# Fifty elementwise instructions move from GpSimd to VectorE, between the output projection and the first pair of the up projection

## The chip, the cores and the metric

The kernel runs on one core of one Trainium2 chip. The metric is device time of one execution in microseconds (us), the median of several runs. The profile shows one more execution, with a record of every instruction. "PE" is TensorE (matrix multiply), "PEld" its weight loads, "DVE" VectorE, "ACT" ScalarE, "POOL" GpSimd, "SP" the engine that issues the DMAs. Each engine takes its instructions strictly in the order of its own queue and stops at one whose operand isn't there yet.

## The reference, cut to what matters

One residual block over 1024 frames of width 1024, in float32:

```
h   = rmsnorm(x) * (1 + scale1(c)) + shift1(c)
x   = x + gate1(c) * (concat(ssd(h), shortconv(h)) @ w_out)     # output projection
h   = rmsnorm(x) * (1 + scale2(c)) + shift2(c)
u   = causal_dwconv(h @ w_up) + bias                            # up projection, 2 x 2816 wide
x   = x + gate2(c) * ((silu(g) * v) @ w_down)                   # g, v = halves of u
out = rmsnorm(x)
```

The change lies in the output projection, the norm behind it, and the start of the up projection.

## The kernel before, in words

**Precision and product.** A float32 product is made of three fast ones. Every operand is split into a high part and a low part (`split`, L112 to L117): ACT copies the source into the rounded high part (L116), then another engine subtracts it from the source, which is the low part (L117). `mm3` (L125 to L127) issues high x high, high x low and low x high. So each 128x512 piece of an operand costs one ACT copy and one subtraction, and PE waits for both.

**Strassen-like blocks.** The output projection and the up projection use seven products in place of eight (`sw_operands`, `product`, L1000 on; `prep`, L535 on). Their operands are sums and differences of blocks: `sub` (L387), `add` (L662), and in `prep` the lines L558 and L561.

**Output projection.** `product(m, 8, ring_o, ...)` walks over eight row blocks i; for each it splits two 128x512 operands (`operand`: one from the mixer's result, one from a weight page "raw"), and issues twelve matmuls. The order of the seven products is m1, m2, m6, m5, m3, m7, m4. In m1 and m2 the weight's subtraction is on GpSimd (`eng=nc.gpsimd`), in the others on VectorE; `m2` also puts one `sub` per block on GpSimd. `later`/`defer` spread other work over the products: loads, the gate (L1056), the squares for the norm, and in m7 the splits of `half0` (L1177), of which every second one is on GpSimd.

**Norm and transposes.** Behind the last product, tiles 4 to 7 of x get their gate (L1223), their sum of squares on ACT (L1142), a reciprocal root in about a dozen tiny VectorE instructions (`rsqrt`, L97 to L106), and a scaled copy (`x_norm`, L1156 to L1159). PE then transposes them (`f_tile`, L1165) and ACT moves them out of PSUM (L1167).

**Up projection.** 22 pairs p of a gate block and a value block. `prep_u(p)` returns a list of small steps on the pair's two weight pages: the sums S1 to S4 and seven splits. For pair 0 they run on GpSimd beside the norm, for pair 1 on VectorE, from pair 2 on the sums run on GpSimd and the splits on VectorE. The right operands T1, T2, T3, B22 and T4 are made once, by `put`, out of the transposed tiles; B22 and T4 are made on GpSimd. Then pair follows pair, each with its products, the causal convolution taps (L1309, L1330) and the product of gate and value (L1333). Beside the first pairs run the sums of the sixth modulation vector (L163), sixteen of them.

**What sets the order.** The code is recorded and a scheduler puts each engine's queue in order before the launch; `tc.high_priority` pulls a step forward. Weight pages come from rings of a few buffers: the DMA into a buffer is issued when its last reader is done.

Of the kernel before, what the change touches and what calls it, by code (L numbers as in the profile page):

```python
# [36 lines left out]
def block_kernel(ctx: ExitStack, tc: tile.TileContext, x, crow, w_adat, w_m, w_z, w_dt,  # L37
                 w_out, w_up, w_down, vecs, rows, fnw, consts, out):
    nc = tc.nc
# [14 lines left out]
    def nm(s):  # L54
        uid[0] += 1
        return f"{s}{uid[0]}"

    def big():
        return pg.tile([P, T], F32, tag="pg", name=nm("pg"))

    def bank():
        return ps.tile([P, 512], F32, tag="ps", name=nm("ps"))

    def hhalf(dt=F32R):
        return ph.tile([P, 512], dt, tag="H", name=nm("H"))

    def hpage():
        return hhalf(), hhalf()
# [7 lines left out]
    def halves(page):  # L76
        return page[:, 0:512], page[:, 512:]
# [35 lines left out]
    def split(hi, lo, src, scale=None, eng=None):  # L113

        if scale is None:
            nc.scalar.activation(hi, src, AF.Copy)  # L116
            (eng or nc.vector).tensor_tensor(lo, src, hi.bitcast(F32), op=ALU.subtract)  # L117
        else:
            nc.scalar.activation(hi, src, AF.Copy, scale=scale)
            nc.vector.scalar_tensor_tensor(lo, src, scale, hi.bitcast(F32), op0=ALU.mult,  # L120
                                           op1=ALU.subtract)
# [125 lines left out]
    for k in range(ND):  # L247
# [3 lines left out]
        for q in range(2):  # L251
            s = slice(q * 512, q * 512 + 512)
            o = bank()
# [42 lines left out]
    o = bank()  # L296
# [34 lines left out]
    o = bank()  # L331
# [7 lines left out]
    o = bank()  # L339
# [46 lines left out]
    def sub(o, i0, i1, eng=None):  # L386
        (eng or nc.vector).tensor_tensor(o, i0, i1, op=ALU.subtract)  # L387
# [130 lines left out]
    wts = {}  # L518

    def w_half():  # L520
        if cur[0] is None:
            n = npage[0]
            npage[0] += 1
            pool, nb = (pv[0], 1) if pv[0] and n % 5 == 4 else (pw, None)
            h, l = [pool.tile([P, 1024], F32R, tag=t, bufs=nb, name=nm(t)) for t in ("wh", "wl")]
            cur[0] = (h[:, 512:], l[:, 512:])
            return h[:, 0:512], l[:, 0:512]
        r, cur[0] = cur[0], None
        return r
# [242 lines left out]
    with tc.high_priority(offset=100):  # L772
        for f in w0:
            f()
        gs, vl = big(), bank()
# [68 lines left out]
    for p in range(1, NS):  # L844
# [3 lines left out]
        gs, vl = (big(), nxt_vl) if p > 1 else (gs1, vl1)  # L848
# [73 lines left out]
    def sc_pair(i, q):  # L922

        rt, s = halves(tpage()), slice(q * 512, q * 512 + 512)
        for h in range(2):
            j = 2 * i + h
            y = Y[8 + j][q]
            nc.sync.dma_start(y, yd[j][:, s])
            for g in range(2):
                nc.sync.dma_start(rt[h][g * 64:(g + 1) * 64, :],  # L930
                                  rd[2 * j + g, s].partition_broadcast(64))
            nc.vector.scalar_tensor_tensor(y, y, col(V_SN + j), rt[h], op0=ALU.mult, op1=ALU.mult)
# [3 lines left out]
    def sw_operands(Y, load, eng=None):  # L936

        def m1(i):
            return Y(i)[0], load(i, 0, 0), []

        def m2(i):
            gl, gr, vl, vr = Y(i)
            return vl, load(i, 0, 1), [lambda: sub(gl, gl, gr, eng), lambda: add(gr, gr, vr)]

        def m5(i):
            gl, gr, vl, vr = Y(i)
            return gr, load(i, 2, 0), [lambda: sub(gr, vr, gl)]

        def m6(i):
            gl, gr, vl, vr = Y(i)  # L950
            return gr, load(i, 3, 1), [lambda: sub(vl, vl, gr, eng)]

        def m3(i):
            return Y(i)[2], load(i, 1, 1), []

        def m7(i):
            return Y(i)[0], load(i, 3, 0), []

        def m4(i):
            return Y(i)[3], load(i, 2, 1), []  # L960
        return m1, m2, m5, m6, m3, m7, m4

    def acc_banks():
        return [bank() for c in range(4)]

    def big_banks():
        return [*halves(big()), *halves(big())]

    def operand(f, i, ring, eng=None):

        h, l = ring()
        a, w, after = f(i)
        split(h[:, 0:512], l[:, 0:512], a)
        split(h[:, 512:], l[:, 512:], w, eng=eng)
        for g in after:
            g()
        return h[:, 0:512], l[:, 0:512], h[:, 512:], l[:, 512:]

    def dmm(o, c, op, start, stop, more=False):
        ah, al, bh, bl = op  # L980
        cs = slice(c * P, (c + 1) * P)
        mm3(o, ah[:, cs], al[:, cs], bh, bl, start, stop, more)
# [3 lines left out]
    def defer(n):  # L986
        for _ in range(min(n, len(later))):
            later.pop(0)()

    def product(f, n, ring, o=None, i0=0, i1=None, pops=1, eng=None, more=False):  # L990

        o = o or acc_banks()
        for i in range(i0, n if i1 is None else i1):
            op = operand(f, i, ring, eng)
            for c in range(4):
                dmm(o[c], c, op, i == 0 and not more, i == n - 1, more)
            defer(pops)
        return o
# [13 lines left out]
    NM2 = 4  # L1012
# [6 lines left out]
    def fetch():  # L1019
        if not quarters:  # L1020
            return
        i, page, half = quarters.pop(0)
        if wq[0] is None:
            t, wq[0] = halves(rawpage())
        else:
            t, wq[0] = wq[0], None
        src = w_out[page, i] if page < 2 else tout[i][page - 2]
        nc.sync.dma_start(t, src[:, half * 512:half * 512 + 512])
        ahead.append(t)

    def load_o(i, page, half):
        fetch()
        return ahead.pop(0)

    def Yo(i):
        return Y[2 * i] + Y[2 * i + 1]

    m1, _, _, _, m3, m7, m4 = sw_operands(Yo, load_o)

    def m2(i):  # L1040
        gl, gr, vl, vr = Yo(i)
        return vl, load_o(i, 0, 1), [lambda: sub(gl, gl, gr, nc.gpsimd)]

    def m6(i):
        gl, gr, vl, vr = Yo(i)
# [13 lines left out]
    def hset():  # L1059
        return [hhalf(F32) for c in range(4)]  # L1060
# [39 lines left out]
    later += [lambda: ssd_load(1, (0, 1)), lambda: ssd_load(1, (2, 3)), last_pair]  # L1100
    later += [lambda: ssd_load(1, (4, 5)), lambda: ssd_load(1, (6, 7))]
    pgs = hhalf(F32)
    o = product(m1, 8, ring_o, i1=7, pops=2, eng=nc.gpsimd)
    later += [lambda i=i: sc_pair(i, 1) for i in range(3)]
    o2 = product(m2, 8, ring_o, big_banks(), i1=NM2, eng=nc.gpsimd)
    op = operand(m1, 7, ring_o)
    for c in range(4):
        dmm(o[c], c, op, False, True)
# [5 lines left out]
    for c in range(4):  # L1114
        nc.scalar.activation(acc[c], o[c], AF.Copy)
    oa = o
    o = product(m2, 8, ring_o, o2, NM2, eng=nc.gpsimd)
    c11 = hset()
    for c in range(4):
        add(c11[c], o[c], acc[c])  # L1120
# [40 lines left out]
    def f_tile(q, k):  # L1161

        o = bank() if q else big()[:, 0:512]
        for i in range(4):
            nc.tensor.transpose(o[:, i * P:(i + 1) * P], xn[4 * q + i][:, k * P:(k + 1) * P], ident)  # L1165
        f = yhalf()
        nc.scalar.activation(f, o, AF.Identity, scale=A2c[:, k:k + 1], bias=sh2[:, k:k + 1])  # L1167
        return f

    xn = [None] * NT  # L1170
    f0, f1 = [None] * ND, [None] * ND

    def half0(k):
        f0[k] = f_tile(0, k)
        o = OPS["B11" if k < 4 else "B21"]
        o[k % 4] = hpage()
        split(o[k % 4][0], o[k % 4][1], f0[k], eng=nc.gpsimd if k % 2 else nc.vector)  # L1177

    for c in range(4):
        later += [lambda c=c: gate(c12[c], c, 1), lambda c=c: x_norm(c)]  # L1180
# [17 lines left out]
    def prep_u(p):  # L1198
        def s3_tile():
            if p == 0:  # L1200
                return s3_first
            return pv[0].tile([P, 512], F32, tag="t3", bufs=1, name=nm("s3"))
        return prep(p, [w_up[2 * p], w_up[2 * p + 1]], s3_tile, p < 1,
                    nc.vector if p == 1 else nc.gpsimd, nc.gpsimd if p == 0 else None)

    w0 = prep_u(0)
    s3_first = yhalf()
# [4 lines left out]
    wts[1] = {}  # L1212
    for n, f in zip(("A11", "A12"), halves(t)):
        wts[1][n] = w_half()
        split(*wts[1][n], f, eng=nc.gpsimd)
    for f in w0[2:5]:
        f()
    w0 = w0[5:]
# [14 lines left out]
    def put(name, k, src, eng=None):  # L1233
        n = nput[0]
        nput[0] += 1
        if n < 8:
            d = hpage()
        elif n < 12:
            d = halves(tpage(F32R))
        elif n == 15:  # L1240
            d = small(F32R), small(F32R)
        else:
            d = yhalf(F32R), yhalf(F32R)
        OPS[name][k] = d
        split(d[0], d[1], src, eng=eng)
# [23 lines left out]
    w1 = prep_u(1)  # L1269
# [20 lines left out]
            put("T3", k, f1[k])  # L1290
        prod(V[0][0], "S3", "T3", 0, True, ks=[k])
    for k in range(4):
        put("B22", k, f1[k + 4], nc.gpsimd)
    for k in range(4):
        sub(f0[k + 4], f0[k + 4], f0[k], nc.gpsimd)
        put("T4", k, f0[k + 4], nc.gpsimd)
    hd = [pd.tile([P, T], F32, name=f"hd{p}") for p in range(NF - 1)]


# [66 lines left out]
    for p in range(NF):  # L1366
        nxt = w1 if p == 0 else prep_u(p + 1) if p + 1 < NF else sum(map(early_operand, range(3)), [])
        vl = V[p][0]
        if p > 1:
            G[p] = big()  # L1370
        gl, gr = halves(G[p])
# [34 lines left out]
    o = acc_banks()  # L1406
# [46 lines left out]
    m1, m2, m5, m6, m3, m7, m4 = sw_operands(Yd, load_d)  # L1453
# [17 lines left out]
    o = product(m1, NQ, ring, o, NE)  # L1471
# [4 lines left out]
    o = product(m2, NQ, ring)  # L1476
# [62 lines left out]
    o = product(m5, NQ, ring)  # L1539
# [3 lines left out]
    o = product(m6, NQ, ring)  # L1543
# [4 lines left out]
    o = product(m3, NQ, ring)  # L1548
# [4 lines left out]
    o = product(m7, NQ, ring)  # L1553
# [6 lines left out]
    o = product(m4, NQ, ring, [big()[:, 0:512], bank(), bank(), big()[:, 0:512]], i1=NQ - NL)  # L1560
# [87 lines left out]
```

## Time and profile before

| what | value |
|---|---|
| median of 3 runs | 1467.11 us (1466.14 to 1467.79) |
| profiled execution, device time | 1469.52 us |
| its span, first to last instruction | 1467.7 us |
| mean granted TensorE clock, share of full | 0.979 |
| busy: PE / DVE / ACT / POOL | 1388.9 / 1176.8 / 731.3 / 309.3 us |

A busy time is the sum of an engine's instructions. PE at 95% means that about 79 us of the span pass without a matmul. The chain of waits names what ended last at each moment; its share by engine is no busy share. An idle time in brackets, as `[6.16 <-ACT wh L116]`, stands in front of the row that it delayed, with the instruction that ended it.

### The profile page before, as it was taken

The numbers are of one execution on the slowest core, as the hardware profiler recorded it, in microseconds if no ns is written. First come the engines' busy times: TensorE is split into PE (matmuls) and PEld (weight loads), VectorE is DVE, ScalarE is ACT, GpSimd is POOL, SyncE is SP. The second block draws the span as 40 slices with busy tenths as digits, with TensorE's granted clock in tenths as the row PEclk, the third lists the DMA queues.
The fourth block names the chain that finished last, engine by engine and source line by source line (L and its number), as shares of the span: only waits on it lengthen the run. The fifth ranks groups of instructions, "written<-read, shape, count | busy, mean of one in ns | idle before, by whom it ended". The sixth has DMA issues, their size and how long they took to land.

```text
span 1467.7 us, 17850 instructions
## 1 busy us (share of the span) xinstructions
PE 1388.9 (95%) x6159; PEld 1113.9 (76%) x6159; DVE 1176.8 (80%) x1882; ACT 731.3 (50%) x1272; POOL 309.3 (21%) x213
## 2 busy tenths in 40 slices
PE   4999999999999999998998699999999999999997
PEld 2788876777777777876886477888888888888885
DVE  7988868978898785599489799777777776889688
ACT  6633365666544434344486453444444444545463
POOL 0000032322012322261014733332333330000000
PEclk9999999999999999999999799999999999999999
DMA  8878964336454431785335132222222222856322
GB/s 319 299 267 316 310 199 164 136 103 222 152 173 154 140 122 61 253 253 184 114 116 172 58 129 101 86 86 82 77 87 86 87 86 101 316 207 209 100 101 101
DMA packets 89723, 232.18 MB, mean 158 GB/s; under 512 B 10296, under 2 KB 11016, under 8 KB 89632
## 3 DMA queue, kind: packets, MB, share of 16 engines
q1 hardware_dynamic: 89584, 231.00, 45.9%
q8 instruction: 48, 0.79, 0.2%
q14 instruction: 43, 0.35, 0.1%
q10 hardware_dynamic: 48, 0.05, 0.0%
HBM read 178.93 MB, written 52.08 MB: 157 GB/s over the span
## 4 chain that ended last, share of the span: by engine, by line
PE 63%; DVE 19%; DMA 6%; issue 5%; ACT 4%; POOL 1%; SPq 0%; DVEq 0%; POOLq 0%; ACTq 0%
PE ps L125 11%; PE ps L126 11%; PE ps L127 11%; PE pg L125 8%; PE pg L126 8%; PE pg L127 8%; DVE wl L117 3%; PE ps L485 2%; DVE sm L835 1%; DMA sm<-in_w_adat 1%; DMA cmb<-in_w_down 1%; ACT wh L116 1%; DVE cmb L387 1%; DVE T L373 1%; PE ps L493 1%
## 5 line engine op out<-in xcount | busy, mean ns | idle before, releaser
L116 ACT ACTIVATE wh<-raw 128x512 fp32r<-128x512 f32 (+1 forms) x272 | 173.0, 656 | 263.6 <-POOL raw L561 142.9
L117 DVE TENSOR_TENSOR wl<-raw,wh 128x512 fp32r<-128x512 f32 (+1 forms) x252 | 212.3, 855 | 78.7 <-ACT wh L116 72.6
L125 PE MATMUL pg<-H,wh 128*128 128x512 f32 x464 | 185.8, 402 | 10.5 <-ACT wh L116 6.2
L127 PE MATMUL pg<-H,wl 128*128 128x512 f32 x464 | 184.0, 397 | 1.7 <-DVE wl L117 1.7
L126 PE MATMUL pg<-H,wh 128*128 128x512 f32 x464 | 184.8, 398 | 0.4 <-DVE H L117 0.4
L125 PEld LDWEIGHTS pg<-H,wh 128*128 128x128 f32 x464 | 88.8, 192 | 32.1 <-ACT wh L116 7.3
L125 PE MATMUL ps<-H,wh 128*128 128x512 f32 x272 | 109.1, 402 | 3.8 <-ACT u L1265 3.8
L558 POOL TENSOR_TENSOR s<-raw,raw 128x512 f32<-128x512 f32 x28 | 53.5, 1912 | 278.4 <-DVE wl L117 166.6
L126 PE MATMUL ps<-H,wh 128*128 128x512 f32 x272 | 109.1, 401 | 3.2 <-DVE H L117 3.2
L127 PE MATMUL ps<-H,wl 128*128 128x512 f32 x272 | 108.0, 397 | 1.5 <-DVE wl L117 1.5
L126 PE MATMUL ps<-rg,rg 128*128 128x512 f32 x274 | 106.8, 390 | 0.0
L127 PE MATMUL ps<-rg,rg 128*128 128x512 f32 x274 | 106.6, 390 | 0.0
L127 PEld LDWEIGHTS pg<-H,wl 128*128 128x128 f32 x464 | 88.7, 191 | 21.5 <-DVE wl L117 3.2
L125 PE MATMUL ps<-rg 128*128 128x512 f32 x274 | 104.8, 390 | 0.0
L126 PEld LDWEIGHTS pg<-H,wh 128*128 128x128 f32 x464 | 88.7, 191 | 20.8 <-DVE H L117 2.5
L561 POOL TENSOR_TENSOR raw<-raw 128x512 f32<-128x512 f32 x58 | 85.9, 1492 | 78.6 <-DVE wl L117 69.1
L116 ACT ACTIVATE rg<-hp 128x512 fp32r<-128x512 f32 x85 | 51.6, 626 | 66.3 <-PE ps L127 46.1
L117 DVE TENSOR_TENSOR rg<-hp,rg 128x512 fp32r<-128x512 f32 x85 | 56.9, 684 | 18.2 <-ACT rg L116 18.0
L1330 DVE SCALAR_TENSOR_TENSOR cv<-ps,vec,cv 128x511 f32<-128x511 f32 (+2 forms) x132 | 67.8, 564 | 1.5 <-ACT cv L1326 1.4
L1309 DVE SCALAR_TENSOR_TENSOR cv<-pg,vec,cv 128x1023 f32<-128x1023 f32 (+1 forms) x44 | 56.2, 1277 | 15.4 <-ACT cv L1304 15.4
L662 DVE TENSOR_TENSOR pg<-pg,u 128x512 f32<-128x512 f32 x68 | 47.2, 694 | 25.3 <-PE pg L127 24.9
L487 POOL TENSOR_TENSOR xq<-xq,rw 128x512 f32<-128x512 f32 x16 | 19.0, 1186 | 221.3 <-issue 134.2
(379 smaller groups left out, 3513.5 us busy)
## 6 DMA issues: line engine op xcount, KB each, us to landing
raw<-in_w_up SPq DMA_DIRECT2D x45, 512.0 KB
raw<-in_w_m SPq DMA_DIRECT2D x36, 512.0 KB
sm<-in_w_adat SPq DMA_DIRECT2D x48, 256.0 KB
hd<-cv SPq DMA_DIRECT2D x21, 512.0 KB
hp<-hd SPq DMA_DIRECT2D x21, 512.0 KB
wr<-tdn SPq DMA_DIRECT2D x33, 256.0 KB
bc<-in_w_adat SPq DMA_DIRECT2D x16, 512.0 KB
seg<-ccd SPq DMA_DIRECT2D x16, 512.0 KB
```

The costliest lines, as they stand in the source:

```text
L116: nc.scalar.activation(hi, src, AF.Copy)
L117: (eng or nc.vector).tensor_tensor(lo, src, hi.bitcast(F32), op=ALU.subtract)
L125: nc.tensor.matmul(o, ah, bh, start=start, stop=False, skip_group_check=more)
L126: nc.tensor.matmul(o, ah, bl, start=False, stop=False, skip_group_check=more)
L127: nc.tensor.matmul(o, al, bh, start=False, stop=stop, skip_group_check=more)
L485: nc.tensor.matmul(y[:, h * HD:(h + 1) * HD], seg[:, h, :], xd[:, h * HD:(h + 1) * HD], start=True, stop=True)
L487: nc.gpsimd.tensor_tensor(hv(xg), hv(xg), rw[:, 2, g * 8:g * 8 + 8].unsqueeze(2).to_broadcast([P, 8, HD]), op=ALU.mult)
L558: sums.tensor_tensor(s3[0], a11, a21, op=ALU.subtract)
L561: return lambda: sums.tensor_tensor(o, i0, i1, op=op)
L662: nc.vector.tensor_tensor(o, i0, i1, op=ALU.add)
L1309: nc.vector.scalar_tensor_tensor(t[:, i:], g[:, :T - i], col(V_FW + (2 - i) * 44 + j), t[:, i:], op0=ALU.mult, op1=ALU.add)
L1330: nc.vector.scalar_tensor_tensor(o, v, col(V_FW + (2 - i) * 44 + j), o, op0=ALU.mult, op1=ALU.add)
```

## The change

Fifty instructions of shape 128x512 go from GpSimd's queue to VectorE's: in the output projection fifteen splits of weights and eight differences in `m2` (four of these eight belong to the product's second call); four splits of `half0`; four sums and seven splits of the weights of pairs 0 and 1; four splits of B22; four differences and four splits for T4. Nothing else is computed, and no amount of data changes. Besides, the first five steps of pair 1's list (its sums and its splits S2 and S1) are called ahead of the steps that make T4. (The list counts pairs from 0; the change's title calls pair 1 the second pair.)

```diff
     def m2(i):
         gl, gr, vl, vr = Yo(i)
-        return vl, load_o(i, 0, 1), [lambda: sub(gl, gl, gr, nc.gpsimd)]
+        return vl, load_o(i, 0, 1), [lambda: sub(gl, gl, gr)]
...
-    o = product(m1, 8, ring_o, i1=7, pops=2, eng=nc.gpsimd)
+    o = product(m1, 8, ring_o, i1=7, pops=2)
...
-    o2 = product(m2, 8, ring_o, big_banks(), i1=NM2, eng=nc.gpsimd)
+    o2 = product(m2, 8, ring_o, big_banks(), i1=NM2)
...
-    o = product(m2, 8, ring_o, o2, NM2, eng=nc.gpsimd)
+    o = product(m2, 8, ring_o, o2, NM2)
...
-        split(o[k % 4][0], o[k % 4][1], f0[k], eng=nc.gpsimd if k % 2 else nc.vector)
+        split(o[k % 4][0], o[k % 4][1], f0[k])
...
         return prep(p, [w_up[2 * p], w_up[2 * p + 1]], s3_tile, p < 1,
-                    nc.vector if p == 1 else nc.gpsimd, nc.gpsimd if p == 0 else None)
+                    nc.vector if p < 2 else nc.gpsimd)
...
-        split(*wts[1][n], f, eng=nc.gpsimd)
+        split(*wts[1][n], f)
...
     for k in range(4):
-        put("B22", k, f1[k + 4], nc.gpsimd)
+        put("B22", k, f1[k + 4])
+    for f in w1[:5]:
+        f()
+    w1 = w1[5:]
     for k in range(4):
-        sub(f0[k + 4], f0[k + 4], f0[k], nc.gpsimd)
-        put("T4", k, f0[k + 4], nc.gpsimd)
+        sub(f0[k + 4], f0[k + 4], f0[k])
+        put("T4", k, f0[k + 4])
```

The queues show where the moved instructions come to stand. VectorE in product m2 of the output projection (wl is a low part, H and ys hold the mixer's result, raw a weight page; - is before, + is now):

```order
 L117 TENSOR_TENSOR wl_5415<-raw_5264,wh_5414 128x512
-L662 TENSOR_TENSOR ys_5058<-ys_5058,ys_5060 128x512
 L117 TENSOR_TENSOR wl_5455<-ys_5047,wh_5454 128x512
+L117 TENSOR_TENSOR wl_5455<-raw_5307,wh_5454 128x512
 L932 SCALAR_TENSOR_TENSOR ys_5046<-ys_5046,vec,T_5326 128x512
+L387 TENSOR_TENSOR ys_5057<-ys_5057,ys_5058 128x512
+L387 TENSOR_TENSOR ys_5045<-ys_5045,ys_5046 128x512
 L117 TENSOR_TENSOR wl_5476<-ys_5051,wh_5475 128x512
```

The weight's low part now stands right behind that of the mixer's result, and an `add` that isn't needed yet has gone further back.

VectorE at the norm of tiles 4 and 5 (H_6584 and H_6617 are gated products, rs the reciprocal root, raw_6550 and raw_6551 the weight pages of pair 0):

```order
 L117 TENSOR_TENSOR wl_6556<-raw_6550,wh_6555 128x512 x2
+L558 TENSOR_TENSOR ys_6554<-raw_6550,raw_6551 128x512
 L1223 TENSOR_TENSOR H_6584<-ps_5070,grow 128x512
+L561 TENSOR_TENSOR raw_6551<-raw_6551 128x512
 L662 TENSOR_TENSOR xa_5442<-xa_5442,H_6584 128x512
+L561 TENSOR_TENSOR raw_6550<-raw_6551,raw_6550 128x512
+L1223 TENSOR_TENSOR H_6617<-ps_5071,grow 128x512
 L1152 TENSOR_TENSOR sq_6451<-sq_6451 128x1
+L561 TENSOR_TENSOR raw_6550<-raw_6550 128x512
```

Pair 0's four sums stand between the steps of the norm, the first of them ahead of the first gate.

VectorE where T4 is made (sm_6951 is a low part of B22; ys_6966 is the low part of the first T4, ys_6378 to ys_6420 become the other three; ps_7005 is pair 0's sum for the right value half, L662):

```order
+L117 TENSOR_TENSOR wl_6719<-raw_6810,wh_6718 128x512
+L117 TENSOR_TENSOR ys_6966<-ys_6367,ys_6965 128x512
+L387 TENSOR_TENSOR ys_6378<-ys_6378,ys_6295 128x512
+L387 TENSOR_TENSOR ys_6409<-ys_6409,ys_6326 128x512
+L387 TENSOR_TENSOR ys_6420<-ys_6420,ys_6337 128x512
+L117 TENSOR_TENSOR ys_6971<-ys_6378,ys_6970 128x512
+L117 TENSOR_TENSOR wl_6961<-s_6954,wh_6960 128x512
+L117 TENSOR_TENSOR ys_6976<-ys_6409,ys_6975 128x512
+L662 TENSOR_TENSOR ps_7005<-ps_6723,p_6906 128x512
```

T4 now stands on VectorE behind pair 1's sums, and most of it ahead of pair 0's sum for the right value half; between the first transposed tile's difference and that sum VectorE's queue holds 41 instructions.

## Rows read from the trace of the kernel before

**Rows 1.** The page: busy time of two engines, and the chain's shares by engine.

```profile
PE 1388.9 (95%) x6159; PEld 1113.9 (76%) x6159; DVE 1176.8 (80%) x1882; ACT 731.3 (50%) x1272; POOL 309.3 (21%) x213
...
PE 63%; DVE 19%; DMA 6%; issue 5%; ACT 4%; POOL 1%; SPq 0%; DVEq 0%; POOLq 0%; ACTq 0%
```

**Rows 2.** Stretches: us, busy and instructions per engine, PE clock, DMA share, GB/s.

```profile
590.00:676.00 86.00, 79.98 (x347) 63.56 (x346) 68.18 (x89) 34.02 (x58) 36.97 (x23) 0.94 0.77 245
676.00:776.00 100.00, 100.00 (x457) 82.41 (x456) 77.23 (x157) 64.12 (x122) 5.34 (x4) 1.00 0.38 132
776.00:842.00 66.00, 49.58 (x193) 37.05 (x192) 54.73 (x95) 35.15 (x61) 41.49 (x26) 0.82 0.36 119
842.00:930.00 88.00, 81.76 (x347) 65.64 (x346) 79.32 (x118) 41.97 (x65) 28.91 (x18) 0.98 0.32 108
```

**Rows 3.** Waits of PE from 590 to 676: us in total, times, longest.

```profile
PE pg L126 <- POOL wl L117: 4.0, 3, 2.2
PE ps L126 <- DVE wl L117: 1.5, 2, 0.9
PE ps L125 <- ACT wh L116: 0.5, 1, 0.5
```

**Rows 4.** Groups of VectorE, 676 to 756, GpSimd idle: busy us, mean ns, idle.

```profile
L117 DVE TENSOR_TENSOR wl<-raw,wh 128x512 fp32r<-128x512 f32 x22 | 15.0, 680 | 0.0
L106 DVE SCALAR_TENSOR_TENSOR rs<-rs,rs 128x1 f32<-128x1 f32 x12 | 1.7, 149 | 0.0
```

**Rows 5.** Timeline (start, us, what): VectorE alone; VectorE and GpSimd together.

```profile
776.30 1.88 DVE L117 TENSOR_TENSOR wl<-raw,wh 128x512 fp32r<-128x512 f32 x3
...
822.90 1.76 DVE L117 TENSOR_TENSOR H<-ys,H 128x512 fp32r<-128x512 f32 x1
824.58 1.77 DVE L561 TENSOR_TENSOR raw<-raw 128x512 f32<-128x512 f32 x1
...
824.08 1.73 POOL L558 TENSOR_TENSOR s<-raw,raw 128x512 f32<-128x512 f32 x1
```

**Rows 6.** Timeline of VectorE, first and last of fifteen long rows, output projection.

```profile
629.11 1.55 DVE L117 TENSOR_TENSOR wl<-ys,wh 128x512 fp32r<-128x512 f32 x1 [0.16 <-issue]
...
667.14 1.74 DVE L117 TENSOR_TENSOR T<-sm,T 128x512 fp32r<-128x512 f32 x1
```

**Rows 7.** Timeline of PE: its two longest waits from 776 to 842, and what follows.

```profile
795.83 0.48 PE L1165 MATMUL ps<-cst,xa 128*128 128x128 f32 x1 [4.21 <-ACT xa L1156]
819.28 0.80 PE L125 MATMUL pg<-H,wh 128*128 128x512 f32 x1 [6.16 <-ACT wh L116]
819.87 0.63 PE L126 MATMUL pg<-H,wh 128*128 128x512 f32 x1
```

**Rows 8.** Timeline of GpSimd, ACT and VectorE around that 6.16 us wait.

```profile
808.80 6.46 POOL L387 TENSOR_TENSOR ys<-ys,ys 128x512 f32<-128x512 f32 x1 [4.24 <-DVE ys L387]
...
816.52 0.63 ACT L116 ACTIVATE ys<-ys 128x512 fp32r<-128x512 f32 x1 [5.40 <-POOL ys L117]
...
818.74 0.86 DVE L117 TENSOR_TENSOR wl<-s,wh 128x512 fp32r<-128x512 f32 x1 [4.59 <-ACT wh L116]
```

**Rows 9.** Timeline of VectorE: first difference, last of 23 rows, pair 0's sum.

```profile
798.50 2.50 DVE L387 TENSOR_TENSOR ys<-ys,ys 128x512 f32<-128x512 f32 x3 [0.57 <-ACT ys L1167]
...
813.46 0.68 DVE L561 TENSOR_TENSOR raw<-raw,raw 128x512 f32<-128x512 f32 x1
...
839.38 0.70 DVE L662 TENSOR_TENSOR ps<-ps,p 128x512 f32<-128x512 f32 x1 [1.39 <-PE ps L127]
```

**Rows 10.** Timeline at the norm: GpSimd's first sum; a tiny VectorE row.

```profile
778.15 1.29 POOL L558 TENSOR_TENSOR ys<-raw,raw 128x512 f32<-128x512 f32 x1 [9.55 <-DMA raw<-in_w_up]
...
787.34 1.04 DVE L106 SCALAR_TENSOR_TENSOR rs<-rs,rs 128x1 f32<-128x1 f32 x1
```

**Rows 11.** Timeline: pair 1's sum on VectorE, and PE's longest later wait.

```profile
851.85 0.68 DVE L662 TENSOR_TENSOR ps<-ps,p 128x512 f32<-128x512 f32 x1
...
902.47 0.50 PE L125 MATMUL ps<-H,wh 128*128 128x512 f32 x1 [3.08 <-ACT u L1265]
```

## The prediction, made before the changed kernel ran

> **What bounds the kernel now.** I read the page first: PE is busy 1388.9 of 1467.7 us, and the chain of waits is PE for 63% and VectorE for 19% [rows 1]. So a gain can only come from places where PE stands still. The table by stretch finds them [rows 2]: PE has no idle time from 676 to 776, but lacks 6.0 us between 590 and 676, 16.4 us between 776 and 842 (and its clock there is 0.82 of full), 6.2 us between 842 and 930. The first three stretches are the ones that the change touches. GpSimd is busy for 37 and 41 us in the two poor ones, and for 5 us in the good one.
>
> Then the groups of VectorE and its timeline. With GpSimd idle, a 128x512 subtraction takes 0.680 us [rows 4], and three in a row take 1.88 us [rows 5], so starts follow each other every 0.60 us ((1.88 - 0.68) / 2: the end of one overlaps the start of the next). With GpSimd at work beside it, the same kind of row takes 1.76 us, starts 1.68 us apart, and GpSimd's own row takes 1.73 us [rows 5], against 1.29 us when VectorE leaves it alone [rows 10]. So while both are busy they pass one instruction each per 1.7 us; VectorE alone would pass both in 1.2 us. That is the core of the forecast: the work on GpSimd isn't a help, each of its rows costs VectorE about 1.1 us, and taken over it costs 0.60.
>
> The Trainium skill, page "SBUF — State Buffer", section "Who interferes with whom", says that a VectorE instruction with two SBUF inputs and a GpSimd instruction that reads SBUF exclude each other for a whole instruction. The trace agrees (1.76 us is about 0.68 plus one GpSimd row). [...]
>
> **The change, part by part.** *Output projection (23 instructions).* From 624 to 676 VectorE has almost no idle time, and fifteen of its rows take 1.55 us or more, the first and last in [rows 6]: about 15 x 1.1 = 16.5 us of blocking. In that time GpSimd runs 20 of the moved rows, now 20 x 0.60 = 12.0 us on VectorE. So VectorE's queue gets 4.5 us shorter, and PE no longer waits for GpSimd at all. PE's waits here are 4.0 us for GpSimd's low parts, 1.5 us for VectorE's and 0.5 us for ACT's [rows 3], 6.0 us together, plus about 1.5 us from eight matmuls at the lower clock behind them (0.94 in rows 2). A step of twelve matmuls takes PE 2.73 us (12 x 0.227, the distance of starts), and VectorE now has 4 to 5 instructions per step, 2.4 to 3.0 us: just enough. Walking the new queue with ACT's copies at PE's pace, one wait remains: the low part of the eighth m2 block comes 1.3 us late. I take 6.0 of the 7.5 us; bounds 2 (a wait of about 1 us per step on the other steps) and 7.5. From 676 to 776 PE is full, and the lead stays.
>
> *half0 (4).* On GpSimd these four cost VectorE about 2 us, now 2.4: nothing.
>
> *Norm (11 instructions: four sums, seven splits).* VectorE runs the four chains of tiny instructions here, and they are the chain that PE waits for (4.21 us, first of [rows 7]). One of them takes 1.04 us instead of 0.15 because GpSimd is in the way [rows 10, 4]; the stretched rows from 778 to 797 add up to about 6 us. The moved rows add 11 x 0.60 = 6.6 us. Nothing gained, perhaps 0.5 us lost. The first sum waits for a DMA, which it did on GpSimd until 778.15 [rows 10]; behind it now stands the first gate, which VectorE began at 778.11, so the new wait costs 0 to 0.6 us. In PE's queue, pair 1's product A12 x B21 now stands between the transposes, in the 4.21 us gap: PE does 2.7 us of work there, which shortens what follows, but only where PE sets the pace.
>
> *T1 to T4 and pair 0 (12 instructions).* This is the largest term. From the first difference at 798.50 to pair 0's sum at 839.38 pass 40.9 us [rows 9]. Up to 813.46 VectorE runs 23 rows without GpSimd hindering it, 0.68 us apart. Then the three stops of [rows 8]: GpSimd's difference takes 6.46 us since VectorE never lets go, ACT waits 5.40 us for the T4 split, VectorE 4.59 us for ACT. Behind it come a dozen VectorE rows at 1.7 us. In the new queue the same stretch is 41 instructions, none beside GpSimd: 41 x 0.60 = 24.6 us at best, 41 x 0.68 = 27.9 us with the small waits for ACT that the first 23 rows have. I take 26.5 us, a gain of 14.4. What is late next is PE: it gets its operands in bursts of three matmuls with gaps of about 2.5 us, and will spend part of this time at the lower clock (it did after both gaps in rows 7); 27 matmuls are left when the last operand arrives, 6.1 us at full clock and up to 11.6 at half. I take 2 us off for that: 12.5. Bounds: 5 (all 27 at half clock, and one stop like ACT's 5.40 us comes back in part) and 16.
>
> *From pair 0's sum to pair 1's.* 851.85 - 839.38 = 12.5 us [rows 9, 11]; the new queue has 20 rows there, 12.0 us, plus up to four GpSimd rows of pair 2 beside them, which the old one had in part too. Nothing.
>
> Sum: 6.0 + 12.5 = 18.5 us. The profiled execution took 1469.5 us (span 1467.7, 1.8 around it), so 1451.0; it is 2.4 us above the median of the runs, so 1448.6 on their scale. I predict **1449 us**.
>
> **The rivals.** *A: PE's clock takes most of the second term.* TensorE's clock is 0.82 from 776 to 842 [rows 2], and behind the 6.16 us wait the matmuls ran for some 8 us at 1.2 GHz, each 0.63 us long [rows 7] and 0.43 us apart, where at full clock they are 0.39 us long. With VectorE handing out operands one by one, PE stays below a third busy for 13 us, and may do all of B22's and T3's products at 1.2 GHz. Then the second term is 5 instead of 12.5, the first 5: 1467 - 10 = 1457. For it: PE's new queue has less filler there, because A12 x B21 went into the earlier gap. Against it: shorter gaps (0.82 us and less, 807 to 812) left the clock up, and most of PE's work there comes in two blocks at the end. The Trainium skill, page "TensorE: Matmul & The Clock Gate", Part 1, says that the lower clock is the resting state and activity lifts it; by that rule this rival holds in full.
>
> *B: the lead grows in the pairs.* PE's 6.2 us of waits between 842 and 930, the longest 3.08 us [rows 11], stand where VectorE is busy 79.3 of 88 us [rows 2]. If VectorE enters the pairs with its queue in order, these go too, and both terms reach their upper ends: 26 us, 1441. Against it: the sixteen modulation sums and GpSimd's sums for pairs 2 and up stay as they are.
>
> *C: it gets slower.* If the long rows of VectorE are not GpSimd's doing (say, the DMA's, which runs at 245 GB/s in the first stretch), they stay long and the moved work comes on top: 32 instructions in the two stretches in which PE waits, 32 x 0.60 = 19 us, less 4.0 us for GpSimd's splits [rows 3] and perhaps 2 of ACT's stop: 13 us slower, 1480. The point from which it decides is a mean distance of 1.0 us between VectorE's 41 rows (40.9 / 41) with GpSimd idle. Against it: from 676 to 756, with DMA at 132 GB/s, no subtraction is above 0.70 us, and in the second stretch DMA is as low (119) and the rows are long.
>
> *D: it is given back.* VectorE is 90% busy from 842 to 930; if the loads of the modulation weights set the pace there, the lead melts before pair 6 and the time is within 3 us of before. Against it: their DMAs are issued when VectorE frees a page, so they move forward with it.
>
> **How the numbers follow.** Forecast 0.57, A 0.20, B 0.13, C 0.05, D 0.05. The forecast's own range is 1445 to 1454. The range goes down to B (1441) and up past A to 1461, where the first term is at its lower bound and the second at 5 less a little; outside lie C, D and the tails. A measurement can tell 0.2% (3 us) from no change. Faster by more than that: the forecast, A and B, 0.90. Within it: D, 0.05. Slower: C, 0.05.
>
> **What would show it.** Right: VectorE's 128x512 rows from 624 to 842 take 0.67 to 0.75 us, with hardly any above 1.5; PE's waits between 590 and 676 sum to 2 us or less; from the first difference to pair 0's sum 25 to 29 us instead of 40.9; GpSimd empty from the mixer to pair 2's sums. Wrong: long VectorE rows without GpSimd (C); the 41 rows done in time but PE at half clock behind them (A); a new stop of VectorE in front of the first gate or of ACT in front of the last scaled copy, where the load for the modulation row now stands in its queue; pairs 2 to 5 taking as much longer as the lead was (D).

## The result, and the profile after

| | us |
|---|---|
| before, median of 4 runs | 1466.6 (1465.0 to 1467.8) |
| after, median of 4 runs | 1442.4 (1440.3 to 1442.9) |
| after to before | 0.983, 95% interval 0.982 to 0.985 |
| predicted | 1449, range 1441 to 1461 |

The change saves some 24 us. The time lies inside the range, near its lower end, 6.6 us below the predicted value. The profiled execution of after took 1440.3 us with a span of 1438.4.

The page of after, as in [rows 1]: TensorE is busy for a larger share of a shorter span, VectorE for less time although it runs 50 instructions more, and GpSimd lost 80 us of work.

```profile
PE 1378.0 (96%) x6159; PEld 1105.9 (77%) x6159; DVE 1168.2 (81%) x1932; ACT 730.7 (51%) x1272; POOL 229.3 (16%) x163
...
PE 67%; DVE 17%; DMA 6%; ACT 4%; issue 4%; POOL 1%; SPq 0%; DVEq 0%; ACTq 0%; POOLq 0%
```

The table by stretch answers to [rows 2], with the same columns; the limits are in after's own time, so each stretch holds a little later work than the same row of before.

```profile
590.00:676.00 86.00, 85.47 (x393) 70.58 (x392) 71.94 (x121) 38.01 (x66) 0.00 (x0) 0.98 0.83 266
676.00:776.00 100.00, 99.88 (x455) 81.86 (x454) 82.46 (x194) 67.83 (x131) 0.00 (x0) 1.00 0.39 134
776.00:842.00 66.00, 59.91 (x244) 44.55 (x243) 60.33 (x101) 41.22 (x67) 13.23 (x9) 0.92 0.30 98
842.00:930.00 88.00, 83.33 (x355) 67.34 (x354) 74.01 (x112) 37.31 (x58) 30.40 (x19) 0.98 0.36 121
```

TensorE lacks 0.5 us in place of 6.0 in the first stretch, 6.1 in place of 16.4 in the third, at a clock of 0.92 in place of 0.82; the fourth, which the change doesn't touch, lacks 4.7.

TensorE's waits from 590 to 676, as in [rows 3]: nothing but this is left.

```profile
PE pg L126 <- DVE wl L117: 0.5, 1, 0.5
```

After's timeline of VectorE at the places of [rows 8 to 11]: the first sum of pair 0 and an ordinary row behind it, the first difference, the longest stop that is left, pair 0's sum, a row beside two sums that GpSimd still has, and pair 1's sum.

```profile
763.09 0.69 DVE L558 TENSOR_TENSOR ys<-raw,raw 128x512 f32<-128x512 f32 x1
763.69 0.69 DVE L1223 TENSOR_TENSOR H<-ps,grow 128x512 f32<-128x512 f32 x1
...
781.39 2.09 DVE L387 TENSOR_TENSOR ys<-ys,ys 128x512 f32<-128x512 f32 x3 [1.47 <-ACT ys L1167]
...
806.83 0.69 DVE L117 TENSOR_TENSOR ys<-ys,ys 128x512 fp32r<-128x512 f32 x1 [1.54 <-ACT ys L116]
...
809.77 0.70 DVE L662 TENSOR_TENSOR ps<-ps,p 128x512 f32<-128x512 f32 x1 [1.04 <-PE ps L127]
...
815.92 1.78 DVE L163 SCALAR_TENSOR_TENSOR ys<-ys,grow 128x512 f32<-128x512 f32 x1
...
824.11 0.68 DVE L662 TENSOR_TENSOR ps<-ps,p 128x512 f32<-128x512 f32 x1
```

From the first difference to pair 0's sum pass 28.4 us (809.77 - 781.39) in place of 40.9, and the rows take 0.68 to 0.70 us. The 1.78 us row stands beside two of GpSimd's sums for pair 2 (815.53 to 818.86). TensorE's timeline has 0.76 and 1.13 us where [rows 7] has 4.21 and 6.16:

```profile
781.41 2.00 PE L1165 MATMUL ps<-cst,xa 128*128 128x128 f32 x12 [0.76 <-ACT ys L1167]
...
796.23 0.80 PE L125 MATMUL ps<-H,wh 128*128 128x512 f32 x1 [1.13 <-ACT H L116]
```

Before the gain is split, a common start is needed. I take the 32 small matmuls of L1068, early in the output projection; five of the 23 instructions moved there lie ahead of them. By line (minimum, median and longest ns, first and last start), before, after, and in a kernel of the next section (the norm alone), which has those five on GpSimd as before has:

```profile
L1068 PE MATMUL pg<-cst,H x32: 165/252/355, 616.5 to 620.1; 128*128 128x2 f32 x32
```

```profile
L1068 PE MATMUL pg<-cst,H x32: 165/251/354, 611.5 to 615.0; 128*128 128x2 f32 x32
```

```profile
L1068 PE MATMUL pg<-cst,H x32: 165/251/353, 611.7 to 616.2; 128*128 128x2 f32 x32
```

After's execution is already 5.0 us ahead there. That is not the change's: the norm alone is as far ahead without it, so executions differ by that much. The spans differ by 29.3 us, so 24.3 arise behind this mark, which is also the difference of the medians. Counted from the mark, the lead is 10.0 us when VectorE begins the first splits of pair 0 (776.30 in [rows 5], 761.28 after), 12.1 at the first difference, 24.6 at pair 0's sum, 22.7 at pair 1's, 24.0 at the last pair's product, 24.3 at the end. Nothing is gained or lost in the pairs taken together.

### The profile page after: what moved, and what is told of

It reads as the page before. It is cut to its first block, busy times and chain, and to the rows that moved or that the text cites. A ratio compares the mean times of both kernels' runs of the same rounds, so it can differ in the third digit from the quotient of the medians.

```text
span 1438.4 us, 17809 instructions
## 1 busy us (share of the span) xinstructions
PE 1378.0 (96%) x6159; PEld 1105.9 (77%) x6159; DVE 1168.2 (81%) x1932; ACT 730.7 (51%) x1272; POOL 229.3 (16%) x163
## 4 chain that ended last, share of the span: by engine, by line
PE 67%; DVE 17%; DMA 6%; ACT 4%; issue 4%; POOL 1%; SPq 0%; DVEq 0%; ACTq 0%; POOLq 0%
PE ps L125 12%; PE ps L126 12%; PE ps L127 12%; PE pg L125 8%; PE pg L126 8%; PE pg L127 8%; DVE wl L117 3%; PE ps L485 2%; DVE sm L835 1%; DMA sm<-in_w_adat 1%; DVE cmb L387 1%; DMA cmb<-in_w_down 1%; DVE T L373 1%; DMA tout<-cmb 1%; DMA raw<-in_w_m 1%
## 5 line engine op out<-in xcount | busy, mean ns | idle before, releaser
L117 DVE TENSOR_TENSOR wl<-raw,wh 128x512 fp32r<-128x512 f32 (+1 forms) x272 | 220.4, 823 | 78.7 <-ACT wh L116 72.9
L561 POOL TENSOR_TENSOR raw<-raw 128x512 f32<-128x512 f32 x56 | 82.7, 1489 | 78.5 <-DVE wl L117 69.1
L125 PEld LDWEIGHTS ps<-H,wh 128*128 128x128 f32 x272 | 52.1, 191 | 22.9 <-ACT u L1265 6.8
L662 DVE TENSOR_TENSOR pg<-pg,u 128x512 f32<-128x512 f32 x68 | 47.1, 693 | 23.0 <-PE pg L127 22.6
```

Source lines behind the costliest of these rows:

```text
L125: nc.tensor.matmul(o, ah, bh, start=start, stop=False, skip_group_check=more)
L561: return lambda: sums.tensor_tensor(o, i0, i1, op=op)
L662: nc.vector.tensor_tensor(o, i0, i1, op=ALU.add)
```

## The experiments

The theory: GpSimd's running, not only its slowness, takes time from VectorE, and TensorE waits for VectorE. The rivals: TensorE lost only by waiting for GpSimd's results; the new place of T4 is what gains; GpSimd's rows cost something only in these two stretches. All ratios are to before on the same chip, where its median was 1466.0 us for the first four kernels, 1463.6 for the next four and 1464.6 for the last four; differences are taken against these. A hundredth is 14.7 us.

| kernel | median us | ratio to before, 95% |
|---|---|---|
| after | 1442.4 | 0.983 (0.982 to 0.985) |
| projection alone | 1455.8 | 0.994 (0.993 to 0.995) |
| all but the projection | 1452.0 | 0.991 (0.990 to 0.993) |
| norm alone | 1462.3 | 0.998 (0.997 to 0.999) |
| after, T4 at its old place | 1444.5 | 0.986 (0.985 to 0.988) |
| after, B22 and T4 on GpSimd | 1450.6 | 0.991 (0.988 to 0.993) |
| after, and multiplications aside | 1452.0 | 0.992 (0.989 to 0.995) |
| after, and fills aside | 1442.4 | 0.985 (0.981 to 0.988) |
| after, all pairs' sums moved | 1432.6 | 0.978 (0.975 to 0.981) |
| the same, state-space sums moved too | 1421.4 | 0.970 (0.968 to 0.971) |
| the same, no GpSimd | 1440.6 | 0.983 (0.981 to 0.984) |
| all pairs' sums and combinations | 1432.3 | 0.978 (0.976 to 0.980) |
| all pairs' sums and the scan | 1446.7 | 0.988 (0.986 to 0.989) |

**The projection alone.** Before, with these lines of the change:

```
-        return vl, load_o(i, 0, 1), [lambda: sub(gl, gl, gr, nc.gpsimd)]
+        return vl, load_o(i, 0, 1), [lambda: sub(gl, gl, gr)]
-    o = product(m1, 8, ring_o, i1=7, pops=2, eng=nc.gpsimd)
+    o = product(m1, 8, ring_o, i1=7, pops=2)
...
```

> The kernel before with only the output projection's 23 instructions moved (the three products' 15 splits and the 8 subtractions of m2). The theory (GpSimd's running holds VectorE's rows at 1.76 us, and TensorE waits for both and then runs low-clock matmuls) takes the projection's share as read from the two traces, some 10 us: 1456.6 (1455.3 to 1458.5), with the waits of TensorE there 0.5 us in place of 6.0 and about 5 us fewer in the same matmuls. Rival 1, the prediction's own size: 6.0, 1460.6. Rival 2, it is only time that the next stretch takes back, because T1 to T4 still wait for GpSimd: 1464 or more.

10.2 us by the medians, 8.9 by the ratio (6.7 to 11.0): as the theory says; the rival of 1464 is excluded, and the prediction's 6.0 lies just below the interval. TensorE's waits from 590 to 676 are 0.7 us, 0.5 of them for VectorE, in place of 6.0.

**All but the projection.** After, with those lines put back.

> The kernel after with the output projection's 23 instructions left on GpSimd: the norm's, the T tiles', pair 0's and pair 1's are moved and T4 is made late. The theory: the rest is worth what the traces show behind the projection, 2.1 for the norm and 12.5 for the T tiles, 14.4 in all: 1452.2 (1450.5 to 1454). First difference to pair 0's sum 28 to 29 us in place of 40.9. Rival, the parts help each other (the T tiles are only fast because the projection ended with VectorE ahead): 1455 or more. Together with the run of the projection alone, the two gains should add up to 24.3 if the parts are independent.

14.0 us by the medians, 12.9 by the ratio (10.8 to 15.1). By line, the 16 differences' first start and the pairs' sums' first start:

```profile
L387 DVE TENSOR_TENSOR ys<-ys,ys x16: 683/686/693, 791.5 to 814.8; 128x512 f32<-128x512 f32 x16
...
L662 DVE TENSOR_TENSOR ps<-ps,p x22: 683/694/700, 819.5 to 1220.2; 128x512 f32<-128x512 f32 x22
```

The stretch takes 28.0 us (819.5 - 791.5), about as in after (28.4). The two parts add up, 24.2 us by the medians and 21.8 by the ratios; the second is lower than the whole, but within the intervals. They don't need each other.

**The norm alone.** Before, with half0's, pair 0's and pair 1's early instructions moved:

```
-        split(o[k % 4][0], o[k % 4][1], f0[k], eng=nc.gpsimd if k % 2 else nc.vector)
+        split(o[k % 4][0], o[k % 4][1], f0[k])
-                    nc.vector if p == 1 else nc.gpsimd, nc.gpsimd if p == 0 else None)
+                    nc.vector if p < 2 else nc.gpsimd)
-        split(*wts[1][n], f, eng=nc.gpsimd)
+        split(*wts[1][n], f)
```

> The kernel before with only the norm's instructions moved: the four odd splits of the first half, pair 0's sums and early split, pair 1's two early splits. The prediction gave this part nothing; the two traces give it 2.1 us. Theory by the traces: 1464.5 (1463 to 1466). Rival by the prediction: 1466.6, since what VectorE gains in the norm it waits for at T1 to T4. A third, that pair 0's sums on VectorE also shorten the T stretch because GpSimd comes empty to B22 and T4: 1462 or less.

By the ratio 2.9 us (1.2 to 4.8): a small gain, not nothing. The expectations at 1464.5 and at 1462 can't be told apart by it.

**T4 at its old place.** After, without the three lines that run pair 1's first steps ahead of T4:

```
-    for f in w1[:5]:
-        f()
-    w1 = w1[5:]
```

> The kernel after with T4 made where before had it, ahead of pair 1's first five steps; all on VectorE. The theory: the engines' sharing carries the gain and the order little; B22 and T4 are 8 rows of 0.68 ahead of pair 1's three sums, so pair 1's operands come up to 5.4 us later: 1442.4 to 1447.8, taken 1444.5. Rival, the order is what gains in the T stretch (GpSimd's 12 rows were only late, not in the way): 1452 or more. The mark is the first wait of TensorE behind pair 0's sum.

By the medians this kernel gains 2.8 us less than after, by the ratios 4.3, and the intervals overlap. TensorE's waits for the first copies of the accumulators, from 770 to 930 in this kernel (7.5 us) and from 780 to 960 in after (5.4):

```profile
PE ps L125 <- ACT u L1265: 7.5, 6, 2.7
```

```profile
PE ps L125 <- ACT u L1265: 5.4, 5, 2.6
```

The order is worth a few us at most, and is not what gains.

**B22 and T4 on GpSimd again, at the late place.**

```
-        put("B22", k, f1[k + 4])
+        put("B22", k, f1[k + 4], nc.gpsimd)
-        sub(f0[k + 4], f0[k + 4], f0[k])
-        put("T4", k, f0[k + 4])
+        sub(f0[k + 4], f0[k + 4], f0[k], nc.gpsimd)
+        put("T4", k, f0[k + 4], nc.gpsimd)
```

> The kernel after, with only B22's four subtractions and T4's eight instructions on GpSimd again, at the late place. Theory (GpSimd beside VectorE holds both back): some 12 rows of VectorE pass at 1.7 us in place of 0.6, ACT's splits of pair 1 wait for them, and TensorE with them: 1447 to 1454, taken 1450. Rival (GpSimd's rows were only in the way because they stood ahead of pair 1's sums; in the late place nobody waits for them): 1442.4 to 1444.

As the theory says: 0.0073 above after, 10.7 us, for twelve rows. The timelines show the stop of [rows 7, 8] again at the new place:

```profile
793.87 6.40 POOL L387 TENSOR_TENSOR ys<-ys,ys 128x512 f32<-128x512 f32 x1 [4.31 <-DVE ys L387]
...
804.28 0.80 PE L125 MATMUL pg<-H,wh 128*128 128x512 f32 x1 [6.15 <-ACT wh L116]
```

**GpSimd at work for nobody.** After, with a scratch whose contents no other engine uses; behind the splits that GpSimd had in the projection stands this:

```
+    def side(h, n):
+        nc.gpsimd.tensor_tensor(scr[:, 0:1], scr[:, 0:1], h, op=ALU.mult)
+        for _ in range(n):
+            nc.gpsimd.tensor_tensor(scr, scr, scr, op=ALU.mult)
```

> The kernel after, and GpSimd runs 23 multiplications of a scratch of 128x512 with itself in the output projection, one or two behind each operand that before gave it, started by a 128x1 instruction that reads the operand; no engine waits for the scratch. Theory (GpSimd's running is what costs VectorE, wait or no wait): 23 rows of 1.1 us lost by VectorE, which runs 72 of 86 us there and so has 14 to spare: VectorE's rows beside it at 1.7 us, the time 1450 to 1462, taken 1454. Rival (TensorE only lost because it waited for GpSimd's results): rows beside it still slower or not, the time 1442.4 to 1444.

In the second kernel the last line is a fill:

```
+            nc.gpsimd.memset(scr, 0.0)
```

> The same with 23 fills of the scratch by a constant in place of the multiplications: GpSimd then writes the memory but reads nothing of it (save in the 128x1 instruction). If the engines share what they read through, VectorE's rows stay at 0.6 to 0.7 us and the time at 1442.4 (1441 to 1444). If any work of GpSimd's on that memory is enough, the rows beside a fill are longer too, in proportion to the fill's duration, and the time lies above 1446.

The multiplications cost 0.0089, 13 us; the fills cost nothing that can be told. One wait is left in both: GpSimd's 128x1 instruction reads an operand, and ACT, which writes a later operand into the same buffer, waits until GpSimd is past it. ACT's waits for GpSimd from 600 to 690, with the multiplications and then with the fills:

```profile
ACT wh L116 <- POOL scr L993: 3.6, 2, 2.0
ACT wh L116 <- POOL scr L991: 2.6, 2, 1.6
```

```profile
ACT wh L116 <- POOL scr L993: 5.9, 4, 1.6
```

That is 6.2 and 5.9 us, so this wait is not what costs 13. What TensorE waits for with the multiplications, from 590 to 690, is VectorE alone, 6.8 us where after has 0.5:

```profile
PE pg L126 <- DVE wl L117: 6.8, 4, 4.1
```

So the reason that the prediction rests on is shown apart from any wait for GpSimd's results. The timeline of VectorE and of GpSimd with the multiplications:

```profile
627.69 2.72 DVE L1103 SCALAR_TENSOR_TENSOR ys<-ys,vec,pg 128x512 f32<-128x512 f32 x4 [1.51 <-PE pg L1099]
...
632.98 0.68 DVE L387 TENSOR_TENSOR H<-H,H 128x512 f32<-128x512 f32 x1
633.58 1.53 DVE L117 TENSOR_TENSOR wl<-H,wh 128x512 fp32r<-128x512 f32 x1
...
635.04 1.52 DVE L117 TENSOR_TENSOR wl<-raw,wh 128x512 fp32r<-128x512 f32 x1
...
628.55 2.16 POOL L993 TENSOR_TENSOR scr<-scr 128x512 f32<-128x512 f32 x2
...
633.19 2.83 POOL L993 TENSOR_TENSOR scr<-scr 128x512 f32<-128x512 f32 x2
```

Beside the two GpSimd rows from 633.19 (1.41 us each) VectorE's take 1.52 and 1.53. But beside those from 628.55, VectorE runs four rows that read an accumulator (`pg`, in PSUM) at their usual distance, four in 2.72 us, and GpSimd's take 1.08 us. So it is not any VectorE row that is held. The same two engines with the fills:

```profile
634.12 0.69 DVE L117 TENSOR_TENSOR wl<-H,wh 128x512 fp32r<-128x512 f32 x1
...
642.84 1.28 DVE L387 TENSOR_TENSOR ys<-ys,ys 128x512 f32<-128x512 f32 x2
...
633.53 7.35 POOL L991 TENSOR_TENSOR scr<-scr,wh 128x1 f32<-128x1 f32 x1 [3.19 <-ACT wh L116]
...
642.38 1.11 POOL L993 MEMSET scr<- 128x512 f32 x2
```

A fill takes 0.55 us, and VectorE's rows beside it stay at 0.68. The 128x1 instruction reads the memory, and it is held for 7.35 us while VectorE goes from row to row. The Trainium skill, page "SBUF — State Buffer", section "Who interferes with whom", says that a VectorE instruction with two SBUF inputs contends with a GpSimd instruction that reads SBUF, and not with one that only writes it. Both halves agree with these rows.

**Going on: the sums of the other pairs.** First the up projection's pairs 2 to 21, then the state-space projection's pairs 4 to 11:

```
-                    nc.vector if p < 2 else nc.gpsimd)
+                    nc.vector)
```

```
-                    nc.gpsimd if p > 3 else nc.vector)
+                    nc.vector)
```

> The kernel after with the sums of the up projection's pairs 2 to 21 on VectorE too (80 rows moved). By the theory VectorE gets 0.6 us more and up to 1.1 us less work for each, so that its busy time falls by up to 40 us; but TensorE runs 210 of 210 us from 930 to 1140, so only its waits of some 4.5 us in pairs 0 to 5 can go: 1438.5 to 1442.4, taken 1440.5. Rival (the sums now stand in VectorE's queue ahead of the convolutions, which give the accumulators back): TensorE waits for VectorE in pairs 2 to 21, 1446 or more.

> The kernel with all of the up projection's sums on VectorE, and the sums of the state-space projection's pairs 4 to 11 too (32 more rows moved, between 400 and 590 us). If VectorE's rows beside GpSimd delay TensorE there as they did in pairs 0 to 5, the ratio to before falls from 0.978 by up to 0.004 (some 4.5 us, the waits of TensorE for ACT's copies of the accumulators behind VectorE's long rows); taken 0.976. Rival (TensorE's waits there are its own chain of products and copies): unchanged at 0.978; or above it, if the sums now stand in VectorE's queue ahead of work that TensorE waits for.

Both are faster than after, 0.978 and 0.970, and by more than I had expected (1440.5 us for the first, 0.976 for the second). The first kernel's stretches from 420 to 600 and from 842 to 930, and then the second's:

```profile
420.00:600.00 180.00, 171.36 (x723) 134.43 (x722) 132.68 (x218) 79.48 (x139) 42.86 (x31) 0.98 0.40 131
842.00:930.00 88.00, 88.00 (x386) 72.11 (x385) 80.46 (x141) 44.01 (x67) 0.00 (x0) 1.00 0.37 129
```

```profile
420.00:600.00 180.00, 180.00 (x785) 144.91 (x784) 143.14 (x262) 86.15 (x149) 0.00 (x0) 1.00 0.46 156
```

In the first, the 4.7 us that TensorE lacked from 842 to 930 in after are gone, out of 7.5 gained over after by the ratios. In the second, the 8.6 us from 420 to 600 go too, and the clock is 1.00 in place of 0.98; the ratio falls by 0.0084, 12.3 us. What TensorE waited for there were mostly ACT's copies of accumulators, which is why I had not put these waits down to GpSimd.

**Where it ends: the scan and the combinations.** With all pairs' sums moved, the scan's 28 multiplications, or ten subtractions of weight pages, or (with the state-space sums) everything:

```
-        nc.gpsimd.tensor_tensor(hv(xg), hv(xg),
+        nc.vector.tensor_tensor(hv(xg), hv(xg),
...
-                nc.gpsimd.tensor_tensor(hv(ns), hv(state[g]), hc(Cd), op=ALU.mult)
+                nc.vector.tensor_tensor(hv(ns), hv(state[g]), hc(Cd), op=ALU.mult)
```

```
-        eng = nc.gpsimd if pages else None
+        eng = None
```

> The kernel with all of the up projection's sums on VectorE and only the scan's 28 multiplications moved as well. Theory (sharing costs VectorE as much as the rows themselves): 0.975 to 0.978. Rival (GpSimd's rows lie in VectorE's idle time in the scan, and the move makes its chain longer): 0.979 or above.

> The kernel with all of the up projection's sums on VectorE and only the combinations' subtractions of the later weight pages (10 rows on GpSimd) moved as well. Nobody on TensorE waits for them: unchanged, 0.977 to 0.979. If it gains over 0.002, GpSimd's rows cost there too.

> As the one before, and the scan's 28 multiplications (1.2 us each on GpSimd) and the combinations' 10 subtractions go to VectorE as well: GpSimd is left with 9 small instructions at the start. Theory (each 128x512 row on GpSimd costs VectorE about as much as or more than the row itself would): never slower than the one before, 0.973 to 0.976. Rival (in the scan TensorE waits for VectorE's chain, and GpSimd's row lies where VectorE's queue is idle, so that it is a real second engine there): 0.978 or above.

The combinations change nothing. The scan's rows are better on GpSimd: moving them costs 0.0093, 13.6 us, so my theory, as I had put it there, fails. The kernel with the scan on GpSimd, by groups from 200 to 370 (busy us, mean ns), its GpSimd line, and its stretch from 200 to 360:

```profile
L460 DVE TENSOR_TENSOR seg<-seg,ccv 128x1024 f32<-128x1024 f32 x14 | 21.7, 1547 | 1.6 <-DMA seg<-ccd 1.6
L472 DVE TENSOR_TENSOR seg<-seg,cb 128x1024 f32<-128x1024 f32 x15 | 21.4, 1425 | 0.3
L490 DVE TENSOR_TENSOR xq<-ps,xq 128x512 f32<-128x512 f32 x16 | 11.0, 690 | 16.3 <-PE ps L485 15.1 <-POOL raw L387 1.2
...
L499 DVE TENSOR_TENSOR sm<-xd,Dec 128x512 f32<-128x512 f32 x13 | 10.1, 777 | 0.0
```

```profile
L487 POOL TENSOR_TENSOR xq<-xq,rw x16: 1042/1044/2024, 182.6 to 345.4; 128x512 f32<-128x512 f32 x16
```

```profile
200.00:360.00 160.00, 152.25 (x758) 115.88 (x758) 137.13 (x192) 97.29 (x219) 46.36 (x35) 0.99 0.43 155
```

The kernel with the scan on VectorE, its groups and the same stretch:

```profile
L472 DVE TENSOR_TENSOR seg<-seg,cb 128x1024 f32<-128x1024 f32 x16 | 20.6, 1286 | 0.5 <-ACT seg L463 0.5
L460 DVE TENSOR_TENSOR seg<-seg,ccv 128x1024 f32<-128x1024 f32 x14 | 18.1, 1291 | 0.0
...
L499 DVE TENSOR_TENSOR sm<-xd,Dec 128x512 f32<-128x512 f32 x13 | 8.8, 680 | 0.0
```

```profile
200.00:360.00 160.00, 144.16 (x705) 110.77 (x703) 134.17 (x202) 96.65 (x211) 15.08 (x8) 0.94 0.41 141
```

GpSimd holds VectorE there by 14 x 0.256 + 15 x 0.139 + 13 x 0.097 = 6.9 us in these three groups. The 28 rows on VectorE are 28 x 0.60 = 16.8 us, 10 more. A GpSimd row costs VectorE a quarter of a microsecond here and not 1.1. Most of L487's rows take 1.04 us, their shortest, so nothing holds them: ten of the sixteen stand beside VectorE rows that read an accumulator, at their usual length, or beside none at all (VectorE waits 15.1 us for TensorE at L490). TensorE lacks 15.8 us of 160 instead of 7.7, and its clock is 0.94 instead of 0.99. With no GpSimd at all, 19 us are lost against the fastest; 13.6 of that is the scan, and the other 5 stay open.

## Why the prediction was right, and where it was too small

*The core* (each row on GpSimd costs VectorE about 1.1 us, on VectorE 0.60) holds in both stretches. It is shown by the multiplications for nobody, which cost 13 us (8.8 to 17.3 by their own interval), no less than the same number of rows gained when they left (8.9).

*Output projection: 6.0 predicted, about 8.5 found.* The waits went as said, 6.0 to 0.5 us, a gain of 5.5. Of the lead of 10.0 us behind this part, 1.5 is not counted as the change's: the small matmuls of L1068 are followed by matmuls at half clock in every profile, and how soon it rises varies. From L1068 to the product behind them (L1088; 631.4 before, 624.9 after) pass 13.4 us in five of the fourteen kernels' profiles and 15.0 in nine. All three with the old projection are among the nine, but so are six with the new one. The 4 us behind the small matmuls (us, busy, clock, DMA) in the projection alone, and in after, where the code of the projection is the same:

```profile
615.80:619.80 4.00, 4.00 (x10) 0.50 0.93 304
```

```profile
615.50:619.50 4.00, 4.00 (x13) 0.65 0.87 288
```

That leaves 10.0 - 1.5 - 5.5 = 3.0 us in which the same matmuls run faster. TensorE's timeline in before, behind its longest wait for GpSimd:

```profile
662.45 0.50 PE L126 MATMUL pg<-wl,wh 128*128 128x512 f32 x1 [2.17 <-POOL wl L117]
662.78 0.40 PE L127 MATMUL pg<-wh,wl 128*128 128x512 f32 x1
...
664.78 0.63 PE L125 MATMUL pg<-wh 128*128 128x512 f32 x1
```

From 663.9 to 667.3 the granted clock is at the lower level, and some eight matmuls of 0.63 us cost 1.5 us more: the prediction's "about 1.5 us from eight matmuls at the lower clock" had the right size. The rest, some 1.4 by my estimate, belongs to the waits themselves. A matmul counts as busy for 0.39 us, though the next one starts 0.23 later when nothing is awaited, and the one behind a wait is followed after 0.33 (662.78 - 662.45), so each of the five waits that went took about 0.27 more than its idle time. The step that was too small is "I take 6.0 of the 7.5 us": it held 1.5 back for a wait of 1.3 at the eighth m2 block, which came as 0.5, and it put the slow restart behind each wait at nothing, so that even its upper bound of 7.5 lay too low. Two counts in that paragraph are a little off and carry no term of the sum: from 624 to 676 the trace has sixteen long rows of VectorE and eighteen moved rows of GpSimd, not fifteen and twenty.

*half0 and norm: nothing predicted, 2.1 found.* The lead is the same behind half0 as ahead of it, so the 2.1 lies in the norm. The moved rows were charged 6.6 us against 6 us of stretched ones. By the marks, the norm takes 20.1 us (761.28 to 781.39) in place of 22.2. With this part alone the gain was 1.2 to 4.8 us. The first sum on VectorE stands at 763.09 without a wait, so the price that I saw for the DMA (0 to 0.6 us) was none. Where exactly the 2 us lie is not settled.

*T1 to T4 and pair 0: 12.5 predicted, 12.5 found* (40.9 to 28.4 us). That it fits to a tenth is luck: VectorE's 41 rows took 27.3 us to the end of the last split (781.39 to 808.73), where 26.5 was taken, and pair 0's sum then waited 1.04 us for TensorE, where 2 was taken. The clock entered in another way too. After's stretch from 796 to 806, and ACT's longest stop there:

```profile
796.00:806.00 10.00, 9.08 (x19) 5.93 (x20) 8.63 (x15) 4.32 (x9) 0.00 (x0) 0.50 0.00 0
```

```profile
805.16 0.63 ACT L116 ACTIVATE wh<-raw 128x512 fp32r<-128x512 f32 x1 [3.17 <-PE ps L126]
```

TensorE runs ten microseconds at 1.2 GHz, and ACT stops 3.17 us for it, where before it stopped 5.40 for GpSimd's row [rows 8]; VectorE's stop of 1.54 us for ACT's copy stands behind that one. Behind before's stop the trace has eight VectorE rows of 1.5 to 1.8 us, not a dozen. One experiment shows that most of the term comes from B22's and T4's twelve rows: put back, they cost 10.7 us.

*From pair 0's sum to pair 1's: nothing.* 14.3 us in place of 12.5, with two of GpSimd's sums for pair 2 beside long rows of VectorE there; the pairs behind gave most of that back.

So the sum is 8.5 + 2.1 + 12.5 = 23.1, and 1.5 of the clock, less 0.3 in the rest: 24.3, where 18.5 was predicted. The 1.5 belongs to the two profiled executions, so that the sum agrees with the medians to a tenth is chance.

*The rivals.* A (half clock in the T stretch) came for ten microseconds, as shown, but not to its price: the second term was 12.5 and not 5, since from 806 on TensorE ran at full clock, and the mean clock of the stretch rose from 0.82 to 0.92. C fell: with GpSimd idle, no row of VectorE's from 624 to 810 takes 1 us, although the DMA moved 266 GB/s in the first stretch, more than before. D fell with the marks. B's time (1441) is nearly what was measured, but not by its mechanism: the pairs did not gain, as their own sums stayed on GpSimd. With these moved too, TensorE's waits in the pairs went, as B had it.

## What to carry to other kernels

An elementwise row with two SBUF inputs on GpSimd is no free help to a busy VectorE: price it at what VectorE loses beside it, and compare with the row's distance on VectorE itself. Do that for each stage: where VectorE mostly reads accumulators or waits, GpSimd is a real second engine, and where it streams sums and splits, it is not. Look for it behind the engine that a wait names: in two other stages TensorE's waits for ACT's copies went when GpSimd's rows did.

## What the runs showed of the hardware

- A GpSimd instruction of 128x1 that reads SBUF took 7.35 us beside a VectorE that ran row after row of 0.68 us, 0.60 apart, and 0.19 at other places; a 128x512 difference took 6.40 us. VectorE was not held by the small one.
- Four of VectorE's rows with an accumulator as one input ran at their distance of 0.66 us beside GpSimd's multiplications, and these at 1.08 us. Fills by GpSimd (0.55 us) cost VectorE nothing.
- A VectorE row need not have two 128x512 inputs to be long beside GpSimd: the scaled copy of L1159, one such input and one 128x1, took 1.53 us at 796.40 in before, beside splits on GpSimd, and 0.48 at the same place in after, with GpSimd idle.
- 32 matmuls of two columns, busy without a gap, were followed by matmuls at 1.2 GHz for some 3 us (to 618.3) in after and some 6 (to 621.7) in the projection alone, whose code is the same there.
